# Two blocks of seven half-size products in place of eight plain up tiles in the first MLP segment, with new orders of steps

## The chip, the cores and the metric

One core of one Trainium2 chip. The metric is the device time of one execution of the whole program in microseconds, as the median of several runs.

## The reference

Two layers over 512 tokens of width 1024, all in float32. Cut to what the change touches, one layer is:

```python
proj = x @ w_in                                    # attention and retention inputs, branch gates
ya = neighbourhood_attention(q_na, k_na, v_na)     # 8 heads of 64
yb = bidirectional_retention(q_r, k_r, v_r, g_r)   # 4 heads, 128 / 256 wide
merged = sigmoid(gate_a) * (ya @ w_branch_a) + sigmoid(gate_b) * (yb @ w_branch_b)
x = layer_norm(ALPHA * x + merged @ w_out)         # LN1

h = x @ w_up                                       # 1024 -> 2 * 2816
h = h[t-1] * conv_w[0] + h[t] * conv_w[1] + h[t+1] * conv_w[2] + conv_b
a, b = split(h)
ffn = (gelu(a) * b) @ w_down                       # 2816 -> 1024
ple = sigmoid(x @ w_ple_gate) * (p @ w_ple_proj)
x = layer_norm(ALPHA * x + ffn + ple)              # LN2
```

## The kernel before

**Products.** Every float32 operand is held as a high half `hi` (a cast on ScalarE) and a low half `lo` (a subtraction on VectorE); one product is three matmuls (`mm3`: high by high, high by low, low by high). Most large products are done as seven products of halves instead of eight (a scheme of Strassen's kind): the kinds are `a`, `c`, `t1`, `t2`, `d`, `t3`, `t4`. Their weight forms are sums of the four quarters of a weight: one buffer is loaded by SP with a quarter and turned into `hi` and `lo`, then POOL issues a DMA that adds another quarter to the same buffer, and so on through `a`, `t1`, `t2`, `t4`; `t3` has a buffer and one addition of its own. The sums of the activation's quarters (`S` steps) are made on VectorE by `vg_sums`, as halves `sh` and `sl`.

**The MLP.** The 22 tiles of 128 gate rows and 22 of up rows go in three segments of 3, 4 and 4 pairs (`SEGS`). A plain up tile (`up_half`, steps `g` and `s`) is 24 matmuls of 128x512 into a bank `gt`, then the convolution, GELU and gating from that bank; with `s` the weights come over POOL's queue. A block (`block`) does four tiles (two of gate, two of up) as seven products of 24 matmuls of 128x256, into banks `u`, `v`, `w`; the seven are joined in SBUF tiles `uh` (ScalarE copies the first into each quarter, VectorE adds or subtracts the next), and the convolution reads `uh`. Before the change the second and third segments have two blocks each (`0a` to `1t4` in `UP_ORDER`), the first segment none: its twelve tiles are all plain. They are mixed with the seven products of the embedding's gate (`x @ w_ple_gate`), whose steps have the bare kinds (`a`, `c`, `t1` ...), with the four `S` steps and with `T`, the transposes of the last token tile of LN1. That mixture is `PG`, worked off by `pg()`. Each segment ends with the down products (`down`).

**The order of the work.** Between the start of the attention stretch and the last up tile, all instructions of a layer are recorded and ordered by a planner in the kernel's own Python. TensorE's jobs follow the written lists (`FILL` for gate and attention steps, `R` and `N` the retention and attention heads, `bb` the retention branch's merge products, `vn` the values, `xn` the residual's load; then `PG` and `UP_ORDER`), in `FILL` with a window of ten jobs in which a later one may go first. The other engines' instructions are sorted by due time, with buffers limited as in `CAP`. `_best` plans several rounds: after each it raises the priority (`boost`) of what TensorE waited for in the plan, and keeps the round whose plan ends first. `SET` holds the settings of the planner for layer 0 (key 1) and layer 1 (key 2); `shake` adds a random part to the due times. What the planner sets is the static order on each engine; on the chip, semaphores alone decide.

All instructions are recorded at one helper, so the profile's rows have one line number; the tile names tell them apart.

Of the kernel before, what the change touches and what calls it, by code (L numbers as in the profile page):

```python
# [17 lines left out]
T = 512  # L18
# [24 lines left out]

FILL_WIN = 10
FILL_AT = (36, 40, 56, 24, 28, 8, 20)
FILL = (tuple('2a 2c 7a 7c 2t1 7t1 7t2 2t2 7d 2d 2t3 7t3 7t4 3a 2t4 8a R0 8c R1 3c R0 3t1 8t1 R1 R0 R1 8t2 8d 8t3 R0 3t2 3d 8t4 3t3 4a R1 3t4 5a R2 4c 4t1 R2 5c R3 R3 5t1 4t2 R2 4d 5t2 R2 R3 5d R3 5t3 4t3 4t4 6a 6c 6t1 N0 N1 6t2 5t4 vn 6d N3 N0 N1 6t3 6t4 vn vn bb0 N2 vn N0 N2 N5 N1 bb2 N2 N3 N4 bb1 N6 N6 N6 N7 N5 N4 bb4 bb5 bb6 N7 N4 bb7 N5 N3 N7 xn bb3'.split()),)*2
ORD = ('vector', 'scalar', 'tensor', 'gpsimd', 'sync')
RESIDENT = {(l, c) for l in range(DEPTH) for c in range(68, 72)}

# [4 lines left out]

TABLES_AT = ('0t4', '1t4')

PG = (tuple("a T c S g g S t1 S g g S t2 g g d g g t3 g g t4 g g".split()),) * 2
PG_EARLY = "a"
RES_DMA = (0, 1)
A_DEEP = (4, 5, 5)  # L60
# [1 line left out]
VG_DEEP = 3  # L62
VG_EARLY = "d"
S_SEQ = ("t1", "d", "t2", "t3")
UP_ORDER = ((tuple('0a g 0t1 0c g 0t2 0d 0t3 g 0t4 1a g 1t1 1c 1t2 1d 1t3 s 1t4 s s s'.split()),) * 2,) * 2

DOWN = ("a", "c", "t1", "t2", "d", "t3", "t4")
CAP = {"unit.u": 30, "xt.xt": 1, "raw.raw": 3, "wsplit.hi": 3, "wsplit.lo": 3, "tmp.t": 6, "bias.tb": 2, "bias.cw": 2, "bias.B": 2, "psum.b": 8}
# [4 lines left out]
AFTER = {"tensor": 0.2, "vector": 0.035, "scalar": 0.035, "gpsimd": 0.035}  # L73
BEFORE = {"tensor": 0.11, "gpsimd": 0.05}
_SET = dict(soon=5, hold=6, reserve=10, load=16, work=25, scale=1.0, spare=2, near=10, seed=0, shake=0.0)
SET = {1: dict(_SET), 2: dict(_SET)}
ROUNDS = 12


# [3 lines left out]
def _up_order(l, s):  # L83

    return UP_ORDER[l][s - 1] if s else PG[l]


def _up_blocks(l, s):

    t0 = 2 * sum(SEGS[:s])  # L90
    return [t0 + 2 * b for b in range(sum(k[0].isdigit() and k.endswith("t4") for k in _up_order(l, s)))]
# [131 lines left out]
class Program:  # L223
# [27 lines left out]
    def emit(self):  # L251
# [17 lines left out]
        jobs = _jobs(self.ops)  # L269
        _dues(jobs)  # L270
        end, order = _best(jobs)
        assert end < 1e9
        segs = {}
# [117 lines left out]
def _dues(jobs):  # L391

    soon = lambda j: SET[j.plan]["soon"] if j.plan else 5

# [30 lines left out]

def _best(jobs, rounds=None):

    best = None
    for j in jobs:
        j.boost = 0.0  # L430
    for _ in range(rounds or ROUNDS):
        end, order = _order(jobs)
        if best is None or end < best[0]:
            best = end, order, {j: (j.start, j.done) for j in jobs}
        if end >= 1e9:
            for j in jobs:
                j.boost *= 0.6
            continue
        free, raise_ = 0.0, {}
        ends = {}  # L440
        for j, _ in order:
            ends.setdefault(round(j.done, 2), []).append(j)
        for j in sorted((j for j, _ in order if j.eng == "tensor"), key=lambda j: j.start):
            gap, cur = j.start - free, j
            free = max(free, j.start + j.dur)
            if gap < 0.08 or not j.plan:
                continue
            for _ in range(14):
                last = max(cur.after, key=lambda a: (a.done, a.seq), default=None)
                if last is None or cur.eng == "tensor" and cur.start - last.done > 0.3:  # L450
                    near = [x for d in range(-30, 1) for x in ends.get(round(cur.start + d / 100, 2), ()) if x.eng != "tensor"]
                    last = near[-1] if near and cur.eng == "tensor" else None
                if last is None or last.eng == "tensor":
                    break
                cur = last
                raise_[cur] = max(raise_.get(cur, 0.0), gap)
        if not raise_:
            break
        for j, g in raise_.items():
            j.boost += 0.6 * g + 0.3  # L460
    for j, (a, b) in best[2].items():
        j.start, j.done = a, b
    return best[:2]
# [5 lines left out]
def _order(jobs):  # L469
# [18 lines left out]
    for e in ENGINES:  # L488
# [19 lines left out]
    while count < total:  # L508
# [5 lines left out]
        for e in ENGINES:  # L514
# [7 lines left out]
            plan, q = segs[0]  # L522
            kn = SET.get(plan)
            if e == "tensor":
# [147 lines left out]
def trunk(tc, wpack, x_nat, x_tr, head, p_tr, rpb, decay, ln_par, ln_col, conv, cos_t, sin_t, dist, xi_d, zd, mask, ident_d, out):  # L672
# [5 lines left out]
    with ExitStack() as es:  # L678
# [109 lines left out]
        def fill_items(l):  # L788
# [509 lines left out]
        for l in range(DEPTH):  # L1298
# [537 lines left out]
            vns = na_v()  # L1836
            for f in FILL[l]:
                if f in heads:
# [286 lines left out]
            def pg():  # L2125
# [342 lines left out]
def _pack(l, w_in, w_ba, w_bb, w_out, w_up, w_down, w_pg, w_pp):  # L2468
# [104 lines left out]
```

## Time and profile before

| | |
|---|---|
| median of 3 runs | 1659.93 us (1659.3 to 1660.0) |
| profiled execution | 1660.66 us, its span 1658.8 us |
| TensorE busy | 1645.4 us, 9477 matmuls in the trace |
| VectorE busy | 1289.4 us |
| ScalarE busy | 986.4 us |
| DMA moved | 344.38 MB |

In the profile, an engine's busy time is the union of its instructions' spans; matmuls overlap each other, so a busy TensorE is not a TensorE at its peak. The rows by group give the count, the total busy time, the mean length of one and the idle time ahead of them with what ended it. The rows of waits give who waited for whom: total, times, longest. The first segment of layer 0 lies at about 448 to 552 us, its second at 585 to 676, its attention stretch at 160 to 390; layer 1's first segment begins at about 1272 us.

### The profile page before, as it was taken

The numbers are of one execution on the slowest core, as the hardware profiler recorded it, in microseconds if no ns is written. First come the engines' busy times: TensorE is split into PE (matmuls) and PEld (weight loads), VectorE is DVE, ScalarE is ACT, GpSimd is POOL, SyncE is SP. The second block draws the span as 40 slices with busy tenths as digits, with TensorE's granted clock in tenths as the row PEclk, the third lists the DMA queues.
The fourth block names the chain that finished last, engine by engine and source line by source line (L and its number), as shares of the span: only waits on it lengthen the run. The fifth ranks groups of instructions, "written<-read, shape, count | busy, mean of one in ns | idle before, by whom it ended". The sixth has DMA issues, their size and how long they took to land.

```text
span 1658.8 us, 24840 instructions
## 1 busy us (share of the span) xinstructions
PE 1645.4 (99%) x9477; PEld 1453.3 (88%) x9477; DVE 1289.4 (78%) x1939; ACT 986.4 (59%) x1470; POOL 263.9 (16%) x312
## 2 busy tenths in 40 slices
PE   9999999999999999999999999999999999999997
PEld 7889999888888898898888899998888888988986
DVE  6757998777877857758876489988789687677688
ACT  6766677844466546356476566778535574563564
POOL 0111212110111111112012112222002011111113
PEclk9999999999999999999999999999999999999999
DMA  8997678775587788889679867788765878888784
GB/s 304 245 263 170 167 162 213 180 211 188 153 252 203 196 254 213 223 234 224 184 222 230 227 147 178 169 213 187 206 224 140 271 193 234 244 185 265 205 198 127
DMA packets 102518, 344.38 MB, mean 208 GB/s; under 512 B 11648, under 2 KB 16256, under 8 KB 102400
## 3 DMA queue, kind: packets, MB, share of 16 engines
q0 software_dynamic: 38736, 138.95, 43.9%
q1 hardware_dynamic: 63664, 203.86, 33.7%
q8 instruction: 74, 1.21, 0.3%
q14 instruction: 44, 0.36, 0.1%
HBM read 315.50 MB, written 25.69 MB: 206 GB/s over the span
## 4 chain that ended last, share of the span: by engine, by line
PE 94%; DVE 3%; issue 1%; ACT 1%; DMA 1%; POOL 0%; DVEq 0%; POOLq 0%; SPq 0%; ACTq 0%
PE gt L260 29%; PE u L260 27%; PE v L260 14%; PE gn L260 8%; PE w L260 7%; PE o L260 2%; PE x L260 1%; PE ns L260 1%; PE na L260 1%; PE pt L260 1%; DVE lo L260 1%; PE s L260 1%; PE tr L260 1%; DMA raw<-in_wpack 0%; DVE xn L260 0%
## 5 line engine op out<-in xcount | busy, mean ns | idle before, releaser
L260 PE MATMUL gt<-x1t,hi 128*128 128x512 f32 x896 | 276.6, 390 | 0.0
L260 POOL DMA_DIRECT2D rawa<-in_wpack x138 | 122.4, 908 | 945.0 <-DVE lo L260 719.2
L260 DVE TENSOR_TENSOR lo<-rawa,hi 128x1024 fp32r<-128x1024 f32 (+1 forms) x182 | 216.3, 1198 | 49.4 <-ACT hi L260 49.4
L260 DVE TENSOR_TENSOR lo<-raw,hi 128x1024 fp32r<-128x1024 f32 x167 | 201.2, 1208 | 61.1 <-ACT hi L260 60.6
L260 ACT CAST hi<-rawa 128x1024 fp32r<-128x1024 f32 (+1 forms) x182 | 185.2, 1029 | 94.9 <-DMA rawa<-in_wpack 82.3
L260 ACT CAST hi<-raw 128x1024 fp32r<-128x1024 f32 x167 | 172.7, 1038 | 60.3 <-DVE R L260 15.2
L260 PEld LDWEIGHTS gt<-x1t,hi 128*128 128x128 f32 x896 | 166.8, 188 | 33.3
L260 PE MATMUL gt<-x1t,lo 128*128 128x512 f32 x448 | 174.5, 389 | 0.0
L260 PEld LDWEIGHTS gt<-x1t,lo 128*128 128x128 f32 x448 | 84.2, 188 | 17.6
L260 PE MATMUL u<-xt,hi 128*128 128x256 f32 x448 | 81.8, 284 | 0.0
L260 PE MATMUL gn<-hi,mt 128*128 128x512 f32 x256 | 80.3, 391 | 0.0
L260 PE MATMUL gt<-ybt,hi 128*128 128x512 f32 x256 | 79.9, 393 | 0.0
L260 ACT ACT_TABLE_LOAD x52 | 66.7, 1283 | 13.1 <-DVE u L260 4.5
L260 PE MATMUL v<-hi,sh 128*128 128x512 f32 x184 | 71.7, 389 | 0.0
L260 PE MATMUL v<-lo,sh 128*128 128x512 f32 x184 | 71.7, 389 | 0.0
L260 PE MATMUL v<-hi,sl 128*128 128x512 f32 x184 | 71.7, 389 | 0.0
L260 PEld LDWEIGHTS u<-xt,hi 128*128 128x128 f32 x448 | 70.0, 192 | 0.2
L260 DVE SCALAR_TENSOR_TENSOR gg<-gt,cw,gg 128x511 f32<-128x511 f32 x56 | 41.9, 748 | 30.5 <-ACT gg L260 29.9
L260 PE MATMUL u<-lo,sh 128*128 128x512 f32 x168 | 65.4, 390 | 0.0
L260 PE MATMUL u<-hi,sh 128*128 128x512 f32 x168 | 65.4, 389 | 0.0
L260 PE MATMUL u<-hi,sl 128*128 128x512 f32 x168 | 65.4, 389 | 0.0
L260 PE MATMUL u<-sh,hi 128*128 128x256 f32 x224 | 63.8, 285 | 0.0
(302 smaller groups left out, 4645.2 us busy)
## 6 DMA issues: line engine op xcount, KB each, us to landing
raw<-in_wpack SPq DMA_DIRECT2D x163, 512.0 KB, 6.0
rawa<-in_wpack POOLq DMA_DIRECT2D x132, 512.0 KB, 6.6
rawa<-in_wpack SPq DMA_DIRECT2D x44, 512.0 KB, 6.4
rawt<-in_wpack SPq DMA_DIRECT2D x44, 512.0 KB, 5.9
rawt<-in_wpack POOLq DMA_DIRECT2D x44, 512.0 KB, 8.4
hi<-in_wpack POOLq DMA_DIRECT2D x40, 512.0 KB, 6.8
lo<-in_wpack POOLq DMA_DIRECT2D x40, 512.0 KB, 5.8
sx<-s_scr SPq DMA_DIRECT2D x32, 512.0 KB, 9.0
```

The costliest lines, as they stand in the source:

```text
L260: r = o.call(*[real(x) for x in o.a], **{k: real(v) for k, v in o.k.items()})
```

## The change

`PG`, in both layers, has two blocks (`0a` to `0t4`, `1a` to `1t4`) and four plain tiles instead of twelve plain tiles. The weights of these eight tiles are packed as quarters of two blocks. The `S` steps stand one after the other behind `T` and `c`, and `0a` stands between `a` and `T`. `FILL`, `UP_ORDER` and the settings of layer 1 are new. `_best` also keeps, for each layer, the priorities of the round in which TensorE's planned waits in that layer were least, and plans one more round with these put together.

In instructions: 384 matmuls of 128x512 go and 672 of 128x256 come. VectorE has 12 more 128x1024 subtractions for weights and 12 more joins in `uh`; ScalarE 12 more casts for weights, 16 more copies into `uh` and 6 table loads fewer; POOL 16 more accumulating DMAs; SP as many DMAs as before.

```diff
-PG = (tuple("a T c S g g S t1 S g g S t2 g g d g g t3 g g t4 g g".split()),) * 2
+PG = (tuple('a 0a T S S c 0c S t1 g g S 1a t2 1c 0t1 0t2 1t1 1t2 0d 0t3 1d 1t3 d 0t4 1t4 g t3 t4 g'.split()),
+        tuple('a 0a T S S c 0c S t1 g g S 1a t2 1c 0t1 0t2 1t1 1t2 0d 0t3 1d 1t3 d 0t4 1t4 g t3 t4 g'.split()))
-UP_ORDER = ((tuple('0a g 0t1 0c g 0t2 0d 0t3 g 0t4 1a g 1t1 1c 1t2 1d 1t3 s 1t4 s s s'.split()),) * 2,) * 2
+UP_ORDER = ((tuple('0a 0t1 0c g g 0t2 0d 1a 0t3 g 0t4 g 1t1 1c 1t2 1d 1t3 s 1t4 s s s'.split()), tuple('0a 0t1 0c g g 0t2 0d 0t3 g 0t4 1a 1t1 1c 1t2 1d 1t3 s g s 1t4 s s'.split())),
...
-SET = {1: dict(_SET), 2: dict(_SET)}
+SET = {1: dict(soon=5, hold=6, reserve=10, load=16, work=25, scale=1.0, spare=2, near=10, seed=0, shake=0.0), 2: dict(soon=5, hold=6, reserve=10, load=17, work=25, scale=1.0, spare=2, near=10, seed=2744, shake=0.4)}
...
-    best = None
+    best, part = None, {}
     for j in jobs:
         j.boost = 0.0
-    for _ in range(rounds or ROUNDS):
+    rounds = rounds or ROUNDS
+    for r in range(rounds + 1):
+        if r == rounds:
+            if not part:
+                break
+            for j in jobs:
+                if j.plan in part:
+                    j.boost = part[j.plan][1][j]
...
+            now = j.plan or now
+            cost[now] = cost.get(now, 0.0) + max(gap, 0.0)
...
-        if not raise_:
+        for p, c in cost.items():
+            if p and (p not in part or c < part[p][0]):
+                part[p] = c, {j: j.boost for j in jobs if j.plan == p}
+        if r == rounds:
             break
```

`FILL` keeps its steps; some are moved; its end `bb6 N7 N4 bb7 N5 N3 N7 xn bb3` has become `bb6 bb7 N3 xn N7 N7`.

**POOL, around the last LayerNorm step ahead of the first segment, layer 0.** POOL's queue carries the accumulating DMAs (`rawa`, `rawt`: a weight buffer that a further piece is added to) and the small power for each token tile's `rstd`. `rawa_4536` and `rawa_4556` belong to the gate block, `rawa_4575` and `rawa_4822` to the two new blocks. Before:

```order
L260 DMA rawa_4536<-in_wpack 128x1024
L260 DMA rawa_4556<-in_wpack 128x1024
L260 TENSOR_TENSOR rstd_4652<-ve_4646,mhalf 128x1
L260 DMA rawa_4536<-in_wpack 128x1024
L260 TENSOR_TENSOR rstd_4714<-ve_4708,mhalf 128x1
L260 TENSOR_TENSOR rstd_4759<-ve_4756,mhalf 128x1
L260 TENSOR_TENSOR rstd_4846<-ve_4843,mhalf 128x1
L260 DMA rawa_4556<-in_wpack 128x1024
L260 DMA rawa_4536<-in_wpack 128x1024
L260 DMA rawa_4556<-in_wpack 128x1024
```

and now:

```order
L263 DMA rawa_4536<-in_wpack 128x1024
L263 DMA rawa_4556<-in_wpack 128x1024
L263 DMA rawa_4575<-in_wpack 128x1024
L263 TENSOR_TENSOR rstd_4659<-ve_4656,mhalf 128x1
L263 DMA rawa_4536<-in_wpack 128x1024
L263 TENSOR_TENSOR rstd_4719<-ve_4713,mhalf 128x1
L263 TENSOR_TENSOR rstd_4764<-ve_4761,mhalf 128x1
L263 DMA rawa_4556<-in_wpack 128x1024
L263 DMA rawa_4575<-in_wpack 128x1024
L263 TENSOR_TENSOR rstd_4869<-ve_4861,mhalf 128x1
L263 DMA rawa_4822<-in_wpack 128x1024
L263 DMA rawa_4536<-in_wpack 128x1024
```

Six accumulates instead of three stand ahead of the fourth `rstd`; the fourth `rstd` follows an accumulate that waits for VectorE's `lo` of the same buffer.

**VectorE, from the fourth token tile's first addition (`xn_4479` with `gn`) to its last, same place.** `lo` is the low half of a weight form, `x1t` a piece of the transposed layer input, `mv`, `ve`, `bn` the LayerNorm's statistics. Before:

```order
L260 SCALAR_TENSOR_TENSOR xn_4479<-xn_4479,gn_4740 128x512
L260 TENSOR_TENSOR x1t_4746<-xf_4685,x1t_4746 128x2x256
L260 BN_STATS bn_4623<-xn_4479 128x6
L260 TENSOR_TENSOR lo_4821<-raw_4723,hi_4804 128x1024
L260 BN_AGGR mv_4834<-bn_4623 128x2
L260 TENSOR_TENSOR x1t_4746<-xf_4692,x1t_4746 128x2x256
L260 TENSOR_SCALAR ve_4843<-mv_4834 128x1
L260 SCALAR_TENSOR_TENSOR xn_4479<-xn_4479,mv_4834,lng_4502 128x1024
L260 TENSOR_TENSOR lo_4854<-raw_4748,hi_4832 128x1024
L260 SCALAR_TENSOR_TENSOR xn_4479<-xn_4479,rstd_4846,lnb_4510 128x512 x2
L260 TENSOR_TENSOR lo_4871<-rawa_4556,hi_4791 128x1024
L260 TENSOR_TENSOR lo_4889<-raw_4806,hi_4864 128x1024
```

and now:

```order
L263 SCALAR_TENSOR_TENSOR xn_4479<-xn_4479,gn_4745 128x512
L263 TENSOR_TENSOR lo_4820<-rawa_4556,hi_4791 128x1024
L263 BN_STATS bn_4645<-xn_4479 128x6
L263 TENSOR_TENSOR lo_4839<-raw_4728,hi_4811 128x1024
L263 BN_AGGR mv_4849<-bn_4645 128x2
L263 TENSOR_TENSOR lo_4851<-rawa_4575,hi_4797 128x1024
L263 TENSOR_SCALAR ve_4861<-mv_4849 128x1
L263 SCALAR_TENSOR_TENSOR xn_4479<-xn_4479,mv_4849,lng_4502 128x1024
L263 TENSOR_TENSOR lo_4871<-raw_4758,hi_4841 128x1024
L263 SCALAR_TENSOR_TENSOR xn_4479<-xn_4479,rstd_4869,lnb_4510 128x512 x2
L263 TENSOR_TENSOR lo_4908<-raw_4785,hi_4853 128x1024
```

Between the two additions there were two subtractions for weights and two pieces of `x1t`; now there are four subtractions for weights, and the pieces of `x1t` stand ahead.

**TensorE, at the end of the attention stretch, layer 0.** `pt` are transposes of an attention head's probabilities `S`, `na` its product with the values, `gt` from `ybt` a merge product of the retention branch, `gt` from `yat` one of the attention branch. Before, the merge products of the retention branch end and those of the attention branch begin:

```order
L260 MATMUL gt_4218<-ybt_2836,hi_3926 128x512 x2
L260 MATMUL gt_4218<-ybt_2836,lo_4006 128x512
L260 MATMUL gt_4218<-ybt_3010,hi_3926 128x512 x2
L260 MATMUL gt_4218<-ybt_3010,lo_4006 128x512
L260 MATMUL gt_4218<-ybt_3039,hi_3926 128x512 x2
L260 MATMUL gt_4218<-ybt_3039,lo_4006 128x512
L260 MATMUL gt_4268<-yat_3772,hi_4154 128x512 x2
L260 MATMUL gt_4268<-yat_3772,lo_4161 128x512
L260 MATMUL gt_4268<-yat_4235,hi_4154 128x512 x2
L260 MATMUL gt_4268<-yat_4235,lo_4161 128x512
```

and now:

```order
L263 MATMUL na_4214<-pt_3801,vn_3656 128x256 x2
L263 MATMUL na_4214<-pt_3822,vn_3688 128x256 x2
L263 MATMUL na_4214<-pt_3822,vn_3669 128x256 x2
L263 MATMUL na_4214<-pt_3801,vn_3643 128x2x128 x2
L263 MATMUL pt_4226<-ident,S_4072 128x128 x4
L263 MATMUL pt_4233<-ident,S_4072 128x128 x4
L263 MATMUL gt_4240<-yat_3832,hi_4159 128x512 x2
L263 MATMUL gt_4240<-yat_3832,lo_4166 128x512
L263 MATMUL gt_4248<-yat_3832,hi_4159 128x512 x2
L263 MATMUL gt_4248<-yat_3832,lo_4166 128x512
L263 MATMUL na_4256<-pt_4238,vn_3656 128x256 x2
L263 MATMUL gt_4261<-yat_3832,hi_4193 128x512 x2
```

Where a whole retention product stood behind the last head, the last head's transposes and products now stand between the first products that read the other heads' `yat`.

More of the change, by code (lines that the diff above doesn't have):

```diff
@@ L45 @@
 FILL_AT = (36, 40, 56, 24, 28, 8, 20)
-FILL = (tuple('2a 2c 7a 7c 2t1 7t1 7t2 2t2 7d 2d 2t3 7t3 7t4 3a 2t4 8a R0 8c R1 3c R0 3t1 8t1 R1 R0 R1 8t2 8d 8t3 R0 3t2 3d 8t4 3t3 4a R1 3t4 5a R2 4c 4t1 R2 5c R3 R3 5t1 4t2 R2 4d 5t2 R2 R3 5d R3 5t3 4t3 4t4 6a 6c 6t1 N0 N1 6t2 5t4 vn 6d N3 N0 N1 6t3 6t4 vn vn bb0 N2 vn N0 N2 N5 N1 bb2 N2 N3 N4 bb1 N6 N6 N6 N7 N5 N4 bb4 bb5 bb6 N7 N4 bb7 N5 N3 N7 xn bb3'.split()),)*2
+FILL = (tuple('2a 2c 7a 7c 2t1 7t1 7t2 2t2 7d 2d 2t3 7t3 2t4 7t4 3a 8a R0 8c R1 3c R0 3t1 8t1 R1 R0 R1 8t2 8d 8t3 R0 3t2 3d 8t4 3t3 4a R1 4c 3t4 5a R2 4t1 R2 5c R3 R3 5t1 4t2 R2 4d 5t2 R2 R3 5d R3 5t3 4t3 6a 6c 6t1 N0 N1 6t2 5t4 vn 6d N3 N1 6t3 4t4 6t4 N0 vn vn bb0 N2 vn bb2 N0 N2 N5 N1 N2 N3 N4 N6 bb3 bb1 N5 N6 N6 N4 bb4 N7 bb5 N4 N5 bb6 bb7 N3 xn N7 N7'.split()),
+        tuple('2a 2c 7a 7c 2t1 7t1 7t2 2t2 7d 2d 2t3 7t3 2t4 7t4 3a 8a R0 8c R1 3c R0 3t1 8t1 R1 R0 R1 8t2 8d 8t3 R0 3t2 3d 8t4 3t3 4a R1 4c 3t4 5a R2 4t1 R2 5c R3 R3 5t1 4t2 R2 4d 5t2 R2 R3 5d R3 5t3 4t3 6a 6c 6t1 N0 N1 6t2 5t4 vn 6d N3 N1 6t3 4t4 6t4 N0 vn vn bb0 N2 vn bb2 N0 N2 N5 N1 N2 N3 N4 N6 bb3 bb1 N5 N6 N6 N4 bb4 N7 bb5 N4 N5 bb6 bb7 N3 xn N7 N7'.split()))
 ORD = ('vector', 'scalar', 'tensor', 'gpsimd', 'sync')
@@ L64 @@
 S_SEQ = ("t1", "d", "t2", "t3")
-UP_ORDER = ((tuple('0a g 0t1 0c g 0t2 0d 0t3 g 0t4 1a g 1t1 1c 1t2 1d 1t3 s 1t4 s s s'.split()),) * 2,) * 2
+UP_ORDER = ((tuple('0a 0t1 0c g g 0t2 0d 1a 0t3 g 0t4 g 1t1 1c 1t2 1d 1t3 s 1t4 s s s'.split()), tuple('0a 0t1 0c g g 0t2 0d 0t3 g 0t4 1a 1t1 1c 1t2 1d 1t3 s g s 1t4 s s'.split())),
+            (tuple('0a 0t1 0c g g 0t2 0d 1a 0t3 g 0t4 g 1t1 1c 1t2 1d 1t3 s 1t4 s s s'.split()), tuple('0a 0t1 0c g g 0t2 0d 0t3 g 0t4 1a 1t1 1c 1t2 1d 1t3 s g s 1t4 s s'.split())))
 DOWN = ("a", "c", "t1", "t2", "d", "t3", "t4")
@@ L438, in _best @@
             continue
-        free, raise_ = 0.0, {}
+        free, raise_, cost, now = 0.0, {}, {}, 0
         ends = {}
@@ L442, in _best @@
             ends.setdefault(round(j.done, 2), []).append(j)
-        for j in sorted((j for j, _ in order if j.eng == "tensor"), key=lambda j: j.start):
+        for j in sorted((j for j, _ in order if j.eng == "tensor"), key=lambda j: (j.start, j.seq)):
             gap, cur = j.start - free, j
             free = max(free, j.start + j.dur)
+            now = j.plan or now
+            cost[now] = cost.get(now, 0.0) + max(gap, 0.0)
             if gap < 0.08 or not j.plan:
```

## The prediction

> **What bounds the kernel now.** I read the page first, then who waits for whom on TensorE, then the chain of work in order of time.
>
> ```profile
> span 1658.8 us, 24840 instructions
> PE 1645.4 (99%) x9477; PEld 1453.3 (88%) x9477; DVE 1289.4 (78%) x1939; ACT 986.4 (59%) x1470; POOL 263.9 (16%) x312
> PEclk9999999999999999999999999999999999999999
> PE 94%; DVE 3%; issue 1%; ACT 1%; DMA 1%; POOL 0%; DVEq 0%; POOLq 0%; SPq 0%; ACTq 0%
> ```
>
> TensorE is busy for 99% of the span at full granted clock, and 94% of the chain that ended last is TensorE. A pipelined TensorE can be "busy" and still idle a little between starts, so the next view asks whether it ever waits. These are all of its waits:
>
> ```profile
> PE u L260 <- DVE p L260: 1.9, 2, 1.4
> PE warm L260 <- DVE warm L260: 1.2, 1, 1.2
> PE tr L260 <- DVE xn L260: 1.2, 3, 0.6
> PE o L260 <- DVE qx L260: 0.4, 2, 0.2
> ```
>
> 4.7 us in 1659: nothing but the number of matmuls and the time of each sets the end. So the change is worth what it takes off TensorE, less what it makes TensorE wait.
>
> **What a matmul costs.** The mean of one in the grouped rows overlaps its neighbours, so I take the spacing from unbroken pieces of the chain:
>
> ```profile
> 142.72 20.16 PE u L260 x168
> 461.63 10.88 PE gt L260 x48
> 616.33 5.75 PE u L260 x48
> ```
>
> The `gt` piece lies in the first MLP segment: plain up tiles, 128x512, 10.88 / 48 = 0.2267 us each. The last `u` piece lies in the second segment, which already has two blocks: 128x256, 5.75 / 48 = 0.1198 us each. The first is 168 of the same half width in one run, 20.16 / 168 = 0.1200 us. The shapes:
>
> ```profile
> L260 PE MATMUL gt<-x1t,hi 128*128 128x512 f32 x896 | 276.6, 390 | 0.0
> L260 PE MATMUL u<-x1t,hi 128*128 128x256 f32 x256 | 46.5, 283 | 0.0
> ```
>
> **The main term.** A plain tile is 8 slices of K by 3 split products, 24 matmuls of 512. A block replaces four of them (96) by seven products of 2 x 4 x 3 = 24 matmuls of 256 (168). Four blocks in the program: 384 x 0.2267 = 87.1 us go, 672 x 0.1200 = 80.6 us come. **TensorE loses 6.4 us.** Halving the width costs 0.1200 / 0.2267 = 0.53 and not 0.50; seven eighths times 1.06 is 0.926, so each block saves 1.6 us of 21.8.
>
> The Trainium skill, page "TensorE: Matmul & The Clock Gate", section "Back-to-back issue gap", speaks against this: it gives a sustained spacing of 131 ns at 512 columns and 81 ns at 128, because every matmul also pays for its weight load. A straight line between these, an estimate from that page, puts 256 columns at three quarters of the price of 512, and seven half products would then cost more than four tiles. This trace, with a weight load for every matmul too, has 0.53, and the row decides.
>
> **A wait that should go.** In the first segment the step `T` transposes the last token tile of the first LayerNorm, right behind the first gate product `a`. Both layers lose time there:
>
> ```profile
> 453.82 0.39 PE L260 MATMUL u<-hi,x1t 128*128 128x512 f32 x1
> 454.76 1.38 PE L260 MATMUL tr<-ident,xn 128*128 128x128 f32 x8 [0.55 <-DVE xn L260]
> 455.90 0.47 PE L260 MATMUL w<-hi,x1t 128*128 128x512 f32 x1
> ...
> 1277.72 0.39 PE L260 MATMUL u<-hi,x1t 128*128 128x512 f32 x1
> 1278.36 1.38 PE L260 MATMUL tr<-ident,xn 128*128 128x128 f32 x8 [0.25 <-DVE xn L260]
> 1279.49 0.48 PE L260 MATMUL w<-hi,x1t 128*128 128x512 f32 x1
> ```
>
> And this is how long the same eight transposes take where they don't wait, 0.80 us from start to next start:
>
> ```profile
> 1265.28 1.04 PE L260 MATMUL tr<-ident,xn 128*128 128x128 f32 x8
> 1266.08 0.48 PE L260 MATMUL gn<-hi,mt 128*128 128x512 f32 x1
> ```
>
> From the last `u` to the first `w`: 2.08 us in layer 0 and 1.77 in layer 1, where 0.23 + 0.80 = 1.03 would do. That is 1.05 + 0.74 = **1.8 us**. The change puts a half-size product, 24 x 0.12 = 2.88 us, between `a` and `T`. What VectorE has to finish by then:
>
> ```profile
> 447.96 0.68 DVE L260 SCALAR_TENSOR_TENSOR xn<-xn,gn 128x512 f32<-128x512 f32 x1
> 453.96 1.41 DVE L260 SCALAR_TENSOR_TENSOR xn<-xn,rstd,lnb 128x512 f32<-128x512 f32 x2
> ```
>
> 7.4 us from the first to the end of the second. The new order drops two half tiles of `x1t` from this stretch (512 wide, 0.68 us as the `uh` row below) and puts two more weight subtractions in (1.22, the `lo` row below): 7.4 - 1.4 + 2.4 = 8.5 us, so to 456.4. TensorE, without a wait, arrives at 454.05 + 2.88 = 456.9. On POOL the `rstd` that the last step needs now stands behind an accumulate:
>
> ```profile
> L260 POOL DMA_DIRECT2D rawa<-in_wpack x138 | 122.4, 908 | 945.0 <-DVE lo L260 719.2
> ```
>
> 0.9 us later, then, while VectorE has an `xn` step and a subtraction to do. The wait goes with half a microsecond to spare; if VectorE is later, between 0 and all of the 1.8 us stays.
>
> **What comes in on the other engines.** Rows of one instruction each:
>
> ```profile
> L260 DVE TENSOR_TENSOR lo<-rawa,hi 128x1024 fp32r<-128x1024 f32 x174 | 211.1, 1221 | 49.4 <-ACT hi L260 49.4
> L260 DVE TENSOR_TENSOR uh<-uh,v 128x512 f32<-128x512 f32 x16 | 11.0, 684 | 25.9 <-PE v L260 25.9
> L260 ACT CAST hi<-rawa 128x1024 fp32r<-128x1024 f32 x174 | 180.5, 1047 | 92.6 <-DMA rawa<-in_wpack 80.0 <-PE v L260 8.7 <-PE o L260 2.1
> L260 ACT ACTIVATE uh<-u 128x512 f32<-128x512 f32 x48 | 28.5, 594 | 48.7 <-PE u L260 48.5
> L260 ACT ACT_TABLE_LOAD x52 | 66.7, 1283 | 13.1 <-DVE u L260 4.5 <-DVE gg L260 4.1 <-DVE sl L260 1.8
> ```
>
> A block prepares seven weight forms where four tiles prepared four, and joins seven results. Per block VectorE gets 3 x 1.22 + 3 x 0.684 = 5.7 us, ScalarE 3 x 1.05 + 4 x 0.594 = 5.5 us; over the program there are six table loads fewer (-7.7 us). All of it is cover, unless VectorE is full:
>
> ```profile
> 160.00:300.00 140.00, 139.75 (x1146) 138.37 (x1146) 130.00 (x245) 103.15 (x168) 30.67 (x37) 1.00 0.74 177
> 448.00:552.00 104.00, 103.35 (x463) 85.40 (x462) 82.14 (x116) 66.13 (x92) 12.78 (x14) 1.00 0.79 223
> 585.00:676.00 91.00, 91.00 (x552) 81.77 (x551) 67.63 (x95) 51.30 (x68) 15.19 (x19) 1.00 0.87 223
> ```
>
> Columns: length, then busy time of PE, weight loads, DVE, ACT, POOL, then clock, DMA share, GB/s. The first MLP segment is the second row. VectorE goes from 82.1 to 93.6 us in a stretch that becomes 104 - 3.2 = 100.8 us: 93%. The first row, where seven such blocks run, has 130.0 / 140 = 93% with TensorE short of the stretch by 0.25 us. So I cost this at nothing; what it costs if the cover goes is the second rival.
>
> **The DMAs.** A block adds four accumulating DMAs (on POOL's queue) and keeps the number of loads.
>
> ```profile
> q1 hardware_dynamic: 4896, 17.04, 44.9%
> q0 software_dynamic: 1872, 6.03, 33.7%
> rawa<-in_wpack POOLq DMA_DIRECT2D x5, 512.0 KB, 5.9
> ```
>
> These are of 448 to 552 us (packets, MB, share of the engines; issue to landing in us); the same queue as in the second row, from 585 to 676 us:
>
> ```profile
> q0 software_dynamic: 2880, 10.49, 57.4%
> ```
>
> In the first segment an accumulating DMA of 0.524 MB takes 0.337 x 104 / (6.03 / 0.524) = 3.05 us of the 16 engines. Eight more are 24.4 us on top of 0.79 x 104 = 82.2: 106.6 us in 100.8. That looks over-full, but the new order issues six of the accumulates ahead of the last LayerNorm step where three stood, so 9 us of it fall into earlier time, and 97 are left. The second segment runs at 87% and with 57.4% of accumulates, without a wait. I cost it at nothing in the forecast; the third rival is the other end.
>
> **The other moves.** The last attention head now ends among the first merge products rather than a whole product ahead of them. The same head's hand-over in the trace:
>
> ```profile
> 364.87 1.04 PE L260 MATMUL pt<-ident,S 128*128 128x128 f32 x8
> 365.56 1.07 ACT L260 CAST pt<-pt 128x512 fp32r<-128x512 f32 x2 [6.12 <-PE pt L260]
> 366.18 1.29 DVE L260 TENSOR_TENSOR pt<-pt,pt 128x512 fp32r<-128x512 f32 x2 [0.42 <-ACT pt L260]
> ```
>
> 1.9 us from the first transposes to the first low half, 2.6 to the second. The new order leaves 0.8 + 6 x 0.2267 = 2.2 and 3.1 us: it fits, by 0.3. The steps of the later segments and layer 1's shaken order are other orders of the same instructions, in stretches where TensorE waits for nothing now. For these seams and the eight half products that stand in a row I allow four waits of 0.2 us, the longest of the `o` row: **0.8 us**; bounds 0 and 3.
>
> **The sum.** The profiled execution took 1660.66 us: the span of 1658.8 and 1.9 around it; it stands 0.73 above the median of 1659.93. 1660.66 - 6.4 - 1.8 + 0.8 = 1653.3 for a profiled run, **1652.5 for the median**.
>
> **The rivals.**
> First, half width at three quarters of the price (the page above, as a mechanism of this kernel: a weight load that no longer hides). 672 x 0.75 x 0.2267 - 87.1 = +27 us, so 1685. The run of 168 at 0.1200 us speaks against it: 1 in 100.
>
> Second, the half products outrun their weights. Each takes 2.88 us of TensorE and needs a cast, a subtraction and a landed accumulate; eight stand in a row (`0t1` to `1t3`), and on VectorE a join that waits for TensorE stands ahead of the next weights. If two of the eight come one join and one subtraction late (0.684 + 1.22 = 1.9 us) in each layer, 7.6 us come back and the result is 1660. For it: VectorE at 93%, and in-order joins. Against: followed along the new order with these durations, the tightest low half is ready 1.8 us ahead of its product. 9 in 100, and 12 more for a milder form, half of it, 1656, which is still faster.
>
> Third, and on the other side: the DMA engines are what ends last in the first segment. If its 106.6 us must be moved in that segment after all, TensorE waits 5.8 us in each layer, most of it late in the eight half products: 1652.5 + 11.6 = 1664. It decides once accumulates land some 2 us later than the 5.9 us of the row. For it: 79% now. Against: 87% and 0 us of waits in the second segment. 5 in 100. The Trainium skill, page "DMA: Bandwidth & Descriptors", section "Where 436 GB/s comes from", puts the limit between HBM and SBUF at about 358 GB/s; the segment would need 27.4 MB in 100.8 us, an estimate of 271 GB/s, so by that rule this rival is out. The time shares above say it is not quite.
>
> Fourth, more waits go: 0.5 us at 1258 us (transposes for `xn`), 0.4 at `o`, and no allowance used: 1650.8. 8 in 100.
>
> **How the numbers follow.** Forecast 65 in 100, around 1652.5. A difference of about 0.2% (3.3 us) is what a measurement of this kernel can tell from none. Faster than that (below 1656.6) are the forecast, the fourth rival and the mild second: 65 + 8 + 12 = 85. Within it: the full second, 9. Slower: the third and first, 6. The range reaches from the fourth rival's end, 1650.5, to 1657.5, past the mild second; above it lie the full second, the third and the first, 15 in 100.
>
> **What would show it.** TensorE should have 9765 or so matmuls, the half-width ones of the first segment spaced 0.120 us; the wait `tr` for `xn` near 0.3 us in total; VectorE near 93% and the DMAs near 95% between 448 and 549 us; no wait of TensorE for `lo` or `hi`. A row of waits of PE `u` or `v` for DVE `lo` of several us would make the second rival right; the same with ACT `hi` waiting for DMA `rawa` or `rawt` just ahead of it, the third. A spacing over 0.13 us would sink the main term.

## The result, and the profile after

The changed kernel takes 1656.04 us (median of 16 runs, 1655.29 to 1657.41) against 1660.02 for the kernel before, measured beside it. The ratio is 0.9976, with a 95% interval of 0.9969 to 0.9984. The forecast was 1652.5. The direction was right, the gain is 4.0 us and not 7.4, and this part of the document is about the missing 3.4.

The profiled run took 1656.36 us, with a span of 1654.6, 4.2 less than before. First the totals of the engines:

```profile
PE 1639.7 (99%) x9765; PEld 1460.0 (88%) x9765; DVE 1309.3 (79%) x1963; ACT 999.1 (60%) x1492; POOL 280.4 (17%) x328
```

TensorE has the 9765 matmuls that were forecast; priced by their mean spacing in the trace (0.2267 and 0.1199 us), they are 6.5 us less than before. The next view is the first MLP segment as one window, from its first product to the first matmul of `down(0)`; layer 0 of the kernel before, then both layers of the kernel after (columns: length, busy PE, weight loads, DVE, ACT, POOL, then clock, DMA share, GB/s):

```profile
448.50:554.00 105.50, 104.85 (x468) 86.55 (x467) 83.64 (x117) 67.19 (x93) 12.78 (x14) 1.00 0.78 219
```

```profile
448.80:550.00 101.20, 101.20 (x610) 90.78 (x609) 84.75 (x114) 68.94 (x99) 18.11 (x20) 1.00 0.92 252
1270.00:1371.20 101.20, 101.20 (x610) 90.78 (x609) 84.55 (x113) 71.66 (x101) 18.24 (x20) 1.00 0.93 257
```

From the first start to the start of `down(0)`, layer 0 is 4.2 us shorter (105.44 to 101.26) and layer 1 3.9 (105.12 to 101.23). Together that is 8.1 us, close to the forecast's 8.2: 6.4 for the matmuls and 1.8 for the wait at `T`. Where that wait was, the timeline of TensorE now shows none:

```profile
457.06 0.28 PE L263 MATMUL u<-x1t,lo 128*128 128x256 f32 x1
457.18 1.03 PE L263 MATMUL tr<-ident,xn 128*128 128x128 f32 x8
457.97 0.47 PE L263 MATMUL w<-hi,x1t 128*128 128x512 f32 x1
```

The transposes start 0.12 us after the last half-width matmul, and `c` 0.79 after them. So the gain was made, and then given back. The waits of TensorE over the whole program say where:

```profile
PE u L263 <- DVE p L263: 1.9, 2, 1.4
PE warm L263 <- DVE warm L263: 1.2, 1, 1.2
PE v L263 <- DVE sl L263: 1.1, 3, 0.5
PE o L263 <- DVE qx L263: 0.7, 1, 0.7
PE tr L263 <- DVE xn L263: 0.6, 1, 0.6
PE v L263 <- ACT sh L263: 0.3, 1, 0.3
PE na L263 <- DVE pt L263: 0.2, 1, 0.2
```

The third row and the last two are new. The last lies in the attention stretch, at 334 us. In the other two, `v` is the step `t1` of `down(0)`, and `sh` and `sl` are the high and low halves of the gated sums `ss` that it multiplies. A wait in this view is shorter than the time that the matmul stream loses, since in the rows a matmul of 512 lasts 0.39 us while the next one starts after 0.2267. Counted from start to start, beyond 0.2267 us for each matmul, `down(0)` lost nothing in either layer before and loses **1.43 us in layer 0 and 2.12 in layer 1** now. Its seven steps took 28.6 us in each layer before, and take 30.0 and 30.7. All other stages together lose some 0.3 us (the first stage gains 0.8 and the fill of layer 1 0.85; the fill of layer 0 loses 0.75, the output product of layer 1 0.73, each merge 0.2). The sum is -6.5 - 1.6 + 3.55 + 0.3 = -4.2, which is the difference of the spans.

Why the sums are late stands in VectorE's timeline. Layer 0 of the kernel after; TensorE's first matmul of `down(0)` starts at 550.03:

```profile
551.91 0.75 DVE L263 SCALAR_TENSOR_TENSOR cb<-gt,cw,cb 128x511 f32<-128x511 f32 x1
...
555.17 1.22 DVE L263 TENSOR_TENSOR sl<-ss,sh 128x1024 fp32r<-128x1024 f32 x1
...
558.45 1.23 DVE L263 TENSOR_TENSOR sl<-ss,sh 128x1024 fp32r<-128x1024 f32 x1
...
561.13 1.23 DVE L263 TENSOR_TENSOR sl<-ss,sh 128x1024 fp32r<-128x1024 f32 x1
```

And in the kernel before, where `down(0)` starts at 553.95:

```profile
549.52 1.53 DVE L260 SCALAR_TENSOR_TENSOR gg<-gt,cw,gg 128x511 f32<-128x511 f32 x2 [2.63 <-ACT gg L260]
...
552.11 2.36 DVE L260 TENSOR_TENSOR sl<-ss,sh 128x1024 fp32r<-128x1024 f32 x2
554.38 0.69 DVE L260 TENSOR_TENSOR lo<-raw,hi 128x512 fp32r<-128x512 f32 x1
554.98 1.53 DVE L260 SCALAR_TENSOR_TENSOR cb<-gt,cw,cb 128x511 f32<-128x511 f32 x2
...
562.70 1.22 DVE L260 TENSOR_TENSOR sl<-ss,sh 128x1024 fp32r<-128x1024 f32 x1
```

The first `cb` row is where VectorE gets at the last plain product, which ends the segment. I call what VectorE does from there to the end of the third `sl` the tail. `down(0)` can do 50 matmuls without the third `sl`: its steps `a` and `c`, 18 each, and the first 14 of `t1`. That is 11.3 us. Before, two of the three `sl` are done ahead of the tail, and VectorE even stood idle for 2.63 us: the tail starts 1.0 us after the product and lasts 8.9 us, done at +10.0. After, all three lie in it: it starts at +1.9 and lasts 10.45 us, done at +12.3, 1.0 too late. In layer 1 the tail starts at +1.0, as before the change, and lasts 12.0 us, so there it is late by what it holds alone. In the queue of layer 0 the first two `sl` stand 3.2 and 2.2 us behind the ends of the ScalarE casts `sh` that they need; the third starts as its `sh` ends. What brings all three into the tail is the order `0t4 1t4 g t3 t4 g`: the two blocks' `t4` stand side by side, 25 and 22 us ahead of the segment's end, and their gating, their sums and the plain pair's all come at once.

```profile
525.00:552.00 27.00, 27.00 (x121) 22.38 (x120) 23.59 (x40) 17.86 (x25) 5.20 (x6) 1.00 0.70 147
```

```profile
475.00:500.00 25.00, 25.00 (x158) 22.68 (x157) 14.72 (x20) 13.86 (x19) 2.63 (x3) 1.00 1.04 310
500.00:525.00 25.00, 25.00 (x189) 24.04 (x189) 19.26 (x22) 16.30 (x19) 3.50 (x4) 1.00 0.83 220
525.00:552.00 27.00, 27.00 (x134) 22.89 (x133) 27.00 (x44) 21.82 (x33) 5.34 (x6) 1.00 0.93 236
```

The row by itself is the kernel before, the three rows are the kernel after. VectorE is busy 23.59 of 27 us before and 27.00 of 27 after, while it has 10 us to spare between 475 and 500. Its share of the whole segment is 84%, and that hides this.

### The profile page after: what moved, and what is told of

Its sections match the earlier page's. It is cut to its first block, busy times and chain, and to the rows that moved or that the text cites. A ratio compares the mean times of both kernels' runs of the same rounds, so it can differ in the third digit from the quotient of the medians.

```text
span 1654.6 us, 25522 instructions
## 1 busy us (share of the span) xinstructions
PE 1639.7 (99%) x9765; PEld 1460.0 (88%) x9765; DVE 1309.3 (79%) x1963; ACT 999.1 (60%) x1492; POOL 280.4 (17%) x328
## 4 chain that ended last, share of the span: by engine, by line
PE 91%; DVE 5%; DMA 2%; issue 1%; ACT 1%; POOL 0%; DVEq 0%; POOLq 0%; ACTq 0%
PE u L263 29%; PE gt L263 22%; PE v L263 15%; PE gn L263 8%; PE w L263 8%; PE o L263 2%; PE x L263 1%; DMA rawt<-in_wpack 1%; DVE lo L263 1%; PE ns L263 1%; PE na L263 1%; PE pt L263 1%; PE s L263 1%; PE tr L263 1%; PE st L263 1%
## 5 line engine op out<-in xcount | busy, mean ns | idle before, releaser
L263 DVE TENSOR_TENSOR lo<-raw,hi 128x1024 fp32r<-128x1024 f32 (+1 forms) x159 | 191.3, 1207 | 55.3 <-ACT hi L263 55.1
L263 PE MATMUL gt<-x1t,hi 128*128 128x512 f32 x640 | 197.5, 390 | 0.0
L263 ACT CAST hi<-raw 128x1024 fp32r<-128x1024 f32 (+1 forms) x159 | 163.9, 1038 | 48.7 <-PE gn L263 17.4
L263 PEld LDWEIGHTS gt<-x1t,hi 128*128 128x128 f32 x640 | 118.9, 188 | 23.7
L263 PE MATMUL gt<-x1t,lo 128*128 128x512 f32 x320 | 124.5, 389 | 0.0
L263 PE MATMUL v<-sh,hi 128*128 128x256 f32 x288 | 81.7, 284 | 0.0
L263 PE MATMUL v<-sh,lo 128*128 128x256 f32 x288 | 81.5, 283 | 0.0
L263 PE MATMUL v<-sl,hi 128*128 128x256 f32 x288 | 81.5, 283 | 0.0
L263 PE MATMUL u<-sl,hi 128*128 128x256 f32 x288 | 81.5, 283 | 0.0
L263 PE MATMUL u<-sh,lo 128*128 128x256 f32 x288 | 81.5, 283 | 0.0
```

Of the source, the lines that this page charges most:

```text
L263: r = o.call(*[real(x) for x in o.a], **{k: real(v) for k, v in o.k.items()})
```

## Experiments

Three theories stood at first. **T**: the missing time is a backlog on VectorE at the end of the first segment. **A**: the new orders and settings elsewhere lose it. **B**: the DMA engines are full in the segment, which has a share of 0.92. The experiments split T into two: the amount of VectorE's work (from there on called T), and the order of its queue (called O).

**The segment alone.** `PG` of the change put into the kernel before; nothing else.

```
-PG = (tuple("a T c S g g S t1 S g g S t2 g g d g g t3 g g t4 g g".split()),) * 2
+PG = (tuple('a 0a T S S c 0c S t1 g g S 1a t2 1c 0t1 0t2 1t1 1t2 0d 0t3 1d 1t3 d 0t4 1t4 g t3 t4 g'.split()), ...
```

> The kernel before with the new order of the first MLP segment (PG) alone; fill order, order of the later segments, settings and the planner's extra round as before. Theory T (the missing 3.4 us are a backlog on VectorE at the end of the first segment, made by the new segment itself): within 1 us of the changed kernel, 1655 to 1657, TensorE waiting 2.5 to 4.5 us in the first down product (both layers together). Theory A (the new orders and settings elsewhere lose it): about 1653, that wait below 1 us. Theory B (DMA engines full in the first segment): 1655 to 1657 as T, but with waits at products whose weights are late, not at the sums.

Measured: 1658.41 us, ratio 0.9993 (0.9984 to 1.0002). None of the three had this. The waits:

```profile
PE u L261 <- DVE p L261: 2.7, 4, 1.1
...
PE v L261 <- DVE lo L261: 0.9, 1, 0.9
PE w L261 <- DVE k L261: 0.7, 1, 0.7
```

By the same count from start to start, `down(0)` loses 0.99 and 1.36 us, and the segment ahead of it another 2.56 and 1.70, for results and weights that VectorE prepares. It is the same engine and the same stretch, with more lost.

**All but the segment.** The changed kernel with `PG` of before.

> The changed kernel with the old first segment (PG of before, twelve plain tiles); all the other orders and settings new. T: 1659 to 1660.5, no wait in the first down product. A: about 1663, slower than before by the missing 3 us. B: as T.

Measured: 1660.36 us, ratio 1.0004 (0.9995 to 1.0013), and nothing lost in `down(0)`. T and B had this; theory A wanted 1663 and falls. But the sum of the two parts is no sum: 0.9993 and 1.0004 make 0.9997, the whole change 0.9976. The new orders are worth nothing on the old segment and 0.0017, some 2.8 us, on the new one. The planner sorts VectorE's queue of a whole layer at once, so a list that is changed in a later segment changes what stands in the first.

**The last plain product earlier.**

```
-... d 0t4 1t4 g t3 t4 g
+... d 0t4 1t4 g g t3 t4
```

> The changed kernel with one step moved: the last plain product of the first segment stands ahead of the steps t3 and t4 of the gate product and no longer behind them (5.4 us of TensorE earlier, by 48 products of 0.2267 us for the two steps, or about 10.9 us if both are whole). T: VectorE can form the plain pair's sums while t3 and t4 run; the wait of the first down product falls from 3.55 us (both layers) to below 1.5, the time to about 1654. B: no change within 0.5 us, since the loads keep their order. A: no change.

Measured: 1658.19 us, ratio 0.9992 (0.9983 to 1.0001), so slower than the change itself, which none of the three had. The third `sl` is now done in time (at 561.27, with `down(0)` from 550.2), but `down(0)` loses 2.54 and 2.50 us, and on other things:

```profile
PE v L263 <- DVE R L263: 1.2, 1, 1.2
...
PE v L263 <- DVE lo L263: 1.2, 1, 1.2
```

These are reads of `v` into the residual `R` (layer 0) and a weight's `lo` (layer 1), which now stand behind the sums and the gates of `t3` and `t4`. T in its first form (make room for the plain pair's sums) was wrong: the wait only changed its name.

**The blocks apart, in one way.**

```
-... 1t1 1t2 0d 0t3 1d 1t3 d 0t4 1t4 g t3 t4 g
+... 1t1 0d 0t3 0t4 1t2 1d 1t3 1t4 d g t3 t4 g
```

> The changed kernel with the same steps, the first block finished ahead of the second: 0d 0t3 0t4 stand ahead of 1t2 1d 1t3 1t4, so one block's gating (about 13 us of VectorE) starts some 14 us earlier, in the stretch from 500 us where VectorE is 77% busy. T: the wait of the first down product below 1.5 us, time about 1654, unless half products then wait for their weights. B: DMA share unchanged in the segment, no gain, 1656. A: no change, 1656.

Measured: 1662.61 us, ratio 1.0017 (1.0008 to 1.0025). The half products now wait for the joins `uh` (2.7 us in three waits), which is the place of the prediction's second rival but not its weights. `down(0)` loses 1.58 and 3.83 us: in layer 0 the sums are late still, and in layer 1 it waits 1.9 us for a weight's `lo`. In the code `t4` of a block adds into the bank that the join of its `t3` has to read first, and here `t4` stands right behind `t3`; in the change's order two or three products lie between them.

**Less work on VectorE, the order kept.** The eight multiplications of `R` by the gate `psg` on 16 columns; the planner still reckons with 512, and the order is the same row for row.

```
-                nc.vector.tensor_mul(R[t][:, c], R[t][:, c], sg)
+                nc.vector.tensor_mul(R[t][:, c][:, :16], R[t][:, c][:, :16], sg[:, :16])
...
-        o.dur = 0.155 + 1.04e-3 * n
+        o.dur = 0.155 + 1.04e-3 * (512 if n == 16 else n)
```

> The changed kernel, every engine's order kept row for row, but the eight multiplications of R by the gate psg in each layer's first segment work on 16 of their 512 columns (left out: the gate on the other 496). That takes about 8 x 0.5 = 4 us of VectorE out of each segment, six of the eight between 534 and 550 us. T (VectorE's backlog sets the wait of the first down product): its 1.43 and 2.12 us go to below 0.3 each and the time falls by 3 to 3.5 us, to about 1652.7. B (the DMA engines): wait and time stay, 1656. A (orders elsewhere): stay, 1656.

Measured: 1654.68 us, ratio 0.9973 (0.9964 to 0.9982). Some 4 us were taken out of each layer (eight rows of 0.69 us became 0.18), and at most 1.4 came back in all; the intervals of this kernel and the changed one overlap. `down(0)` still loses 1.07 and 1.99 us. VectorE's timeline of layer 0:

```profile
548.12 1.22 DVE L263 TENSOR_TENSOR lo<-raw,hi 128x1024 fp32r<-128x1024 f32 x1
550.40 0.75 DVE L263 SCALAR_TENSOR_TENSOR cb<-gt,cw,cb 128x511 f32<-128x511 f32 x1 [1.07 <-ACT cb L263]
...
559.62 1.23 DVE L263 TENSOR_TENSOR sl<-ss,sh 128x1024 fp32r<-128x1024 f32 x1
```

VectorE now waits 1.07 us for the last product. The tail begins 1.5 us earlier, 1.0 behind the start of `down(0)`, and takes the same 10.45 us (550.40 to 560.85). So the backlog ahead of the tail did count in layer 0: the third `sl` is now only 0.1 us too late, and half of what `down(0)` loses is a new wait, for a weight's `lo` at 574 us. In layer 1, where no backlog stood ahead of the tail, almost nothing was won: there the tail itself counts.

**The same work on GpSimd.**

```
-                nc.vector.tensor_mul(R[t][:, c], R[t][:, c], sg)
+                nc.gpsimd.tensor_tensor(R[t][:, c], R[t][:, c], sg, ALU.mult)
```

> The changed kernel with those eight multiplications on GpSimd, which is 17% busy; nothing left out. A GpSimd step of this size took 1.34 us in the trace, and accumulating DMAs are queued behind it. The order is planned anew with that. T: the same relief of VectorE as with the narrow gate, minus what late accumulates cost: 1653 to 1655. B: accumulates issued up to 2.7 us later make it worse, 1657 or more.

Measured: 1670.41 us, ratio 1.0064 (1.0052 to 1.0077). T's answer is out. B's "1657 or more" covers the number but not what happened: TensorE's long waits here are for `k` (6.2 us in two) and `p` (5.1 in five, where the changed kernel has 1.9), not for weights. The order was planned anew, so not all of the 14 us need be the move itself. More in the last section.

**One block in place of two** (`one_block`), with nine plain products where eight belong: one surplus product of 24 matmuls in each layer.

```
+PG = (tuple('a 0a T S S c 0c S t1 g g S t2 0t1 0t2 g g 0d 0t3 g d g 0t4 g t3 g t4 g'.split()),
```

> The changed kernel with one block and eight plain tiles in the first segment of both layers in place of two blocks and four. The matmul floor falls by half, 3.2 us below before. T: VectorE gets half of the extra 11.5 us and one block's gating is done in time; the T wait is gone (1.8 us); waits of the first down product below 1 us in both layers together: 1655.5, as fast as two blocks. A: no better than half of the changed kernel's gain, 1658. B: 1655.5 as T.

Measured: 1666.2 us, ratio 1.0040 (1.0027 to 1.0053), and `down(0)` loses nothing. With the surplus product taken out (`... 0t4 g t3 t4 g`):

> One block and eight plain products in the first segment. The kernel called one_block had nine by a slip, 24 surplus products of 0.2267 us in each layer, 10.9 us of its 1666.2. Without them it should take 1655.3, with waits in the first segment as there, 0.4 us in both layers together. Under O the tail behind a last plain product costs nothing here, since only one block's sums fall into it; under T likewise. Over 1657 both would be wrong.

Measured: 1659.60 us, ratio 1.0000 (0.9992 to 1.0009): a miss by 4.3 us, and by the forecast's own words both T and O are wrong as they were put there. `down(0)` loses 1.62 and 1.67 us, although only one block's sums are made and they are done ahead of the tail:

```profile
552.53 0.75 DVE L263 SCALAR_TENSOR_TENSOR cb<-gt,cw,cb 128x511 f32<-128x511 f32 x1
...
558.46 1.22 DVE L263 TENSOR_TENSOR lo<-rawa,hi 128x1024 fp32r<-128x1024 f32 x1
559.60 1.22 DVE L263 TENSOR_TENSOR lo<-raw,hi 128x1024 fp32r<-128x1024 f32 x1
560.73 0.68 DVE L263 TENSOR_TENSOR lo<-rawa,hi 128x512 fp32r<-128x512 f32 x1
561.34 0.68 DVE L263 TENSOR_TENSOR lo<-raw,hi 128x512 fp32r<-128x512 f32 x1
561.94 1.22 DVE L263 TENSOR_TENSOR lo<-rawt,hi 128x1024 fp32r<-128x1024 f32 x1
563.07 1.22 DVE L263 TENSOR_TENSOR sl<-ss,sh 128x1024 fp32r<-128x1024 f32 x1
```

Five weight subtractions, 4.6 us, stand between the pair's last sum and its `sl`. The tail is 11.8 us long, though the other two `sl` are out of it. ScalarE's `sh` for it was done at 559.64, so the queue held it by 3.4 us, twice what TensorE lost: here the order alone makes a wait of the same size.

**Layer 1 without its random part.** `SET[2]` made equal to `SET[1]`, which also puts `load` from 17 to 16.

> The changed kernel with the settings of layer 1 set to those of layer 0 (no random part in the planner's choices, load 16). T: layer 1 behaves as layer 0 or worse; time 1656 to 1658. A: if the shaken order is what lost 2.12 us at layer 1's first down product, that falls to 1.4 and the time to 1655.3.

Measured: 1664.07 us, ratio 1.0024 (1.0015 to 1.0032). In layer 1 the segment loses 6.56 us in place of 0.25, first in two waits of 1.5 us for a weight's `hi` and `lo`; 2.5 of the 6.56 are slower matmuls behind these waits (see the last section). `down(0)` loses 1.96, much as before, but on a weight's `hi` and no longer on the sums. So the settings of layer 1, which the forecast had as "other orders of the same instructions", make 8 us of the time, and T and A both miss it.

**Less work and the product ahead together.** The earlier kernel with the last plain product ahead, with the narrow gate, its order kept row for row.

> The kernel with the last plain product ahead of t3 and t4, its own order kept row for row, with the eight gate multiplications per layer's first segment on 16 of 512 columns (left out: the gate on the other 496). The narrow gate alone took 1.4 us off, because VectorE then stood waiting for the last plain product (1.07 us idle at 550.4 us): the tail behind that product decided there. Here that product ends 11 us earlier. If the amount of VectorE work is the bound (theory T), the 6.3 us of TensorE waits in the two segments fall by 4 us or more, to about 1654. If it is VectorE's order in the tail, whatever stands ahead (theory O), they fall by 1.5 us or less, to about 1657.

Measured: 1657.47 us, ratio 0.9985 (0.9976 to 0.9994). In layer 1 `down(0)` loses 0.49 us in place of 2.50: there the amount was what counted. In layer 0 it loses 4.00 in place of 2.54: 2.4 in and right behind a new wait of 1.6 us for a `hi` whose `rawt` landed late, and 1.4 in slower matmuls behind that, so there a load takes over. Neither forecast fits both layers.

**The blocks one by one, and the plain product ahead.**

```
-... t1 g g S 1a t2 1c 0t1 0t2 1t1 1t2 0d 0t3 1d 1t3 d 0t4 1t4 g t3 t4 g
+... t1 g g S t2 0t1 0t2 1a 0d 0t3 1c 0t4 1t1 1t2 1d 1t3 d 1t4 g g t3 t4
```

> Two blocks, one finished before the other: 0t4 stands five half products ahead of where it stood, both plain products of the last pair ahead of t3 and t4. VectorE's gating of the first block (some 13 us) moves into the stretch from 500 us on, 59 to 77% busy in the changed kernel. T: the waits of PG and the first down product, 4.1 us in both layers, fall to 2 or less: 1654. O: the sums of the first block leave the tail, 2.4 us of sl and 3 us of ss: the wait falls likewise. If half products run out of weights instead (as when the blocks were taken apart before, 1662.6), 1660 or more.

Measured: **1654.36 us**, ratio 0.9967 (0.9955 to 0.9979), the fastest full kernel of the study. It was not timed beside the changed kernel; against the same kernel before, the intervals of the two overlap. `down(0)` loses nothing in layer 0 and 0.16 us in layer 1. VectorE in layer 0, where `down(0)` starts at 550.30:

```profile
553.36 2.35 DVE L263 TENSOR_TENSOR sl<-ss,sh 128x1024 fp32r<-128x1024 f32 x2
...
558.97 1.21 DVE L263 TENSOR_TENSOR sl<-ss,sh 128x1024 fp32r<-128x1024 f32 x1
```

The third `sl` is done 9.9 us after the last product, some 1.5 us in time. This kernel does the change's work, with the same 9765 matmuls and 1963 VectorE instructions, and VectorE is as full:

```profile
525.00:552.00 27.00, 26.67 (x129) 22.24 (x128) 27.00 (x43) 22.38 (x33) 7.13 (x8) 1.00 0.80 194
```

Again 27.00 of 27. The amount is the same and the wait is gone, so here the order made the difference. Not all of the 3.4 us in `down(0)` reach the end: the two segments lose 0.9 us more than in the changed kernel, and layer 1's output product waits 1.5 us for a weight's `lo` at 1246 us.

**The fourth corner**: one by one, the last plain product behind `t3` and `t4`.

> The fourth corner: blocks one by one, with the last plain product behind t3 and t4 again, as in the changed kernel. Either move alone gave no gain so far (the plain product ahead alone: 1658.2) or was not tried alone in this form. If the tail behind that product costs by itself (theory O, as with one block and eight plain tiles: 1.5 us for the last sums in each layer), the first down product waits 3 us in both layers together and the time is about 1657. If only the blocks' own late sums fill the tail, the wait is below 0.5 and the time 1654.5.

Measured: 1661.45 us, ratio 1.0011 (1.0002 to 1.0020), slower than either answer. `down(0)` loses 2.52 us in layer 0, most of it in one wait of 1.7 us for ScalarE's `k`, and 0.03 in layer 1; the segment itself loses 2.26 and 3.88, for weights and results of VectorE. A last plain product at the end need not cost (layer 1), and it moved waits of 6 us into places where the kernel with the product ahead had 1.5.

What this leaves: in the changed kernel the wait comes from VectorE's queue, where the sums stand too far back when the segment ends. As much work in another order goes without it (one by one), and in layer 1 the kept order with less work nearly does too (0.49 us), so order and amount both move it. A late load shows up only in other kernels. No run moved the sums alone in VectorE's queue with all else row for row; that would be the direct test. Which list makes which order is not settled. Each edit of `PG` makes the planner sort the queues anew, and the time lies anywhere between 1654.4 and 1662.6 us for lists that hold the same steps. What the new fill order and the new order of the later segments each add to the new segment was not tried apart.

## Why the prediction was right, and where it was short

- **The matmuls, -6.4 us: right.** The count and the spacing of 0.120 us held; by those the stream's length falls by 6.5 us.
- **The wait at `T`, -1.8 us: right.** The segment's own losses fall from 1.22 and 0.90 us to 0.28 and 0.25, so 1.6. But it was close: VectorE was done with `xn` at 457.39 us, not at 456.4 as the prediction had it, about 0.2 us ahead of the transpose that reads it. The wait `tr` for `xn` that is left, 0.6 us where near 0.3 was foretold, lies ahead of the segment, at 1255 us.
- **Half products outrunning their weights: rightly set aside for this order.** In the changed kernel TensorE has no wait for `lo` or `hi` in the segment. With one by one and the product last it has, up to 1.3 us; with the blocks apart it waits for the joins.
- **The DMAs at nothing: right.** Their share is 0.92 and 0.93 where some 95% was foretold, and 1.04 between 475 and 500 us without a wait of TensorE. The one late load showed up only in a kernel that shifted the steps.
- **VectorE as cover, "I cost this at nothing": the step that failed.** The share was taken over the whole stretch, 93%, and compared with a stretch that runs at 93%. In truth it is 84%: VectorE works only 1.2 and 0.9 us more in the two segments than before, and 4.1 and 5.5 more in `down(0)` behind them. That is the trouble: VectorE cannot do early what TensorE gives it late. The new order was followed for the eight half products and for `T`, not to the first user of the blocks' results. It costs 3.55 us.
- **The allowance, +0.8 us with a bound of 3: too small.** It was for small seams, and all other stages came to some 0.3 us; the 3.55 lie at a place that it did not have in view, beyond its bound by half a microsecond.
- **The later orders and the seed, costed at nothing: right as a sum, wrong as a reason.** Alone they change nothing that can be measured. With the new segment they are worth some 2.8 us, and with layer 0's settings in layer 1 the same lists are 8 us slower.
- **The result lies where the mild second rival stood, 1656, by another mechanism.** It named weights for the half products; it was the sums behind them. The engine, VectorE, was right. That the range reached to 1657.5 for this rival's sake, and so took in a loss that nobody had in view, was luck.

## What to carry to other kernels

When work on an engine that isn't the bound is counted as covered, don't stop at its share of a stretch: follow each new result to its first reader, and count what stands in that engine's queue from the moment its input is ready to the moment it is read. Two units of work that end together hand their follow-up to one queue at once; let one end early enough that its follow-up is done before the last input arrives. Here that paid in one order of three that tried it; in the other two (1662.6 and 1661.5 us) other waits came up. Where a planner sorts the queues, a change to one list is a change to all of them, so parts of a change that are measured alone do not add up.

## What the chip showed that was not expected

GpSimd, though 17% busy, was no place for eight multiplications of 512 columns. The timeline of the kernel that puts them there, GpSimd first, then VectorE:

```profile
545.49 11.64 POOL L263 TENSOR_TENSOR R<-R,psg 128x512 f32<-128x512 f32 x4 [0.61 <-ACT psg L263]
```

```profile
551.97 1.77 DVE L263 TENSOR_TENSOR lo<-raw,hi 128x512 fp32r<-128x512 f32 x1
553.67 2.31 DVE L263 TENSOR_TENSOR sl<-ss,sh 128x1024 fp32r<-128x1024 f32 x1
```

Four of them took 11.64 us, where GpSimd's other rows of this size (`R` with `lnb`, 128x512) take 1.27 us each (the 1.34 of the expectation is a mean over three shapes). All sixteen of the kernel (shortest, median and longest in ns, then first and last start):

```profile
L263 POOL TENSOR_TENSOR R<-R,psg x16: 1309/1736/6017, 474.0 to 1381.2; 128x512 f32<-128x512 f32 x16
```

The first of the four took 6.0 us, while VectorE worked through eleven instructions at their usual lengths. The next three took 1.7, 1.7 and 2.3, and now VectorE's `sl` took 2.31 us in place of 1.22 and a `lo` of 512 columns 1.77 in place of 0.69, each 1.1 us longer. The two engines slow each other down, so the work moved was paid on both, and TensorE waited 3.3 us at one place of `down(0)` in layer 0. The Trainium skill, page "Trainium Architecture — The Big Picture", section "What this means for kernel authors", says that VectorE and GpSimd contend for a shared pair of ports, as an exclusive lock. The rows agree that they contend, and look like taking turns; that ports are the cause they do not tell.

A long wait can cost twice. In layer 0 of the kernel with less work and the product ahead, TensorE lost 2.4 us around the late `hi` between 573.0 and 576.0 us, and the seven matmuls after it took 0.20 us more each. The windows of that kernel show the granted clock, the third figure from the end, before and after:

```profile
571.00:574.50 3.50, 2.40 (x11) 1.67 (x9) 1.23 (x1) 1.23 (x2) 0.00 (x0) 1.00 1.08 307
574.50:580.00 5.50, 4.79 (x13) 3.57 (x14) 4.37 (x8) 2.01 (x3) 0.00 (x0) 0.69 1.07 277
```

It falls from 1.00 to 0.69, which is 1.4 us on top of the wait. The kernel with the gates on GpSimd shows the same behind its wait of 3.3 us (0.76 between 563 and 570 us), so does layer 1 of the kernel with the blocks apart, behind its wait for `lo` (0.50 between 1394.1 and 1397.5 us), and layer 1 of the kernel without the random part (0.55 between 1346 and 1353 us). How long a wait must be the runs do not settle: TensorE also lost 2.4 us at 1367 us in layer 1 of the GpSimd kernel, and the clock stayed at 1.00 between 1370 and 1380 us. The changed kernel's waits in `down(0)` are 0.5 us at most, and the clock of its windows stays at 1.00.
